# A hybrid decoder step on one Trainium2 core: post-norm weight products on GpSimd, and a longer first yield of decode

## The chip, the cores and the metric

The kernel runs on one core of one Trainium2 chip. The metric is the device time of one execution in microseconds (us), taken as the median of several runs. The engines are named as the profile names them: PE (TensorE, the matrix engine; its weight loads are PEld), DVE (VectorE), ACT (ScalarE), POOL (GpSimd) and SP (SyncE, which here only issues DMAs). All data are fp32; PE gets each fp32 operand as a high and a low part (tiles that end in `h` and `l`), so that one product in fp32 is three matmuls.

## The reference

One decoder layer, for a prompt of 2048 tokens (16 blocks of 128) and for 8 sequences of 4 new tokens each that continue from a stored state ("decode", 32 tokens, called the sample chunk):

```python
def rms_norm(x, g):
    y = xf * lax.rsqrt(jnp.mean(xf * xf, axis=-1, keepdims=True) + EPS)
    return (y * g.astype(F32)).astype(x.dtype)

def decoder_layer(x, p, lp, state):
    xn = rms_norm(x, lp['norm_mix_pre'])
    ... # one projection to both groups of heads: mLSTM and sliding-window attention
    mix = jnp.concatenate([y_m, y_a], axis=-1) @ lp['w_out']
    x = x + rms_norm(mix, lp['norm_mix_post'])
    u = rms_norm(x, lp['norm_ffn_pre'])
    f = jnp.square(jax.nn.relu(u @ lp['w_up'])) @ lp['w_down']
    x = x + rms_norm(f, lp['norm_ffn_post'])
    x = x + jax.nn.sigmoid(x @ lp['w_pgate']) * (p @ lp['w_pproj'])
```

The change concerns the factors `norm_mix_post` and `norm_ffn_post` of the two post-norms, and the place of decode's mLSTM and attention in the program.

## The kernel before

The first part (up to some 720 us) projects all blocks and runs the prompt's mLSTM and window attention. The second part goes over three groups, `gi` = 0, 1, 2, of two chunks each: blocks 0-2 and 3-5, 6-8 and 9-11, 12-13 and 14-15 (with the sample chunk in the last group). For each group stand, in this order: `mix_mm` of the first chunk (product with `w_out`, tiles `mo`), `mix_post` (residual, store to `x1d`, norm, transposes `ut<block>...t`), the same for the second chunk, then `mlp` in 16 steps (products `up`, squared ReLU, split into `hh` and `hl`, products `dn`, which DVE accumulates in `f` at L1728), and last the gate (`gate_embed`, `gate_post` with transposes `xt<block>...t`, `gate_mm` with tiles `pg` and `pv`, output put at L1810). The first two steps of `mlp` are direct products; from the third on `up_both` uses a Strassen-like scheme that needs sums of the chunks' operands. `sums()` and `last_sum()` (L1641 to L1675) make them on DVE and POOL, with ACT splitting off the high parts.

PE's order is set by the code: a class `Flow` issues matmuls in program order, and four side generators are advanced at each step of PE's model time. A `yield us` in a generator means that it goes on only once PE's issued work has grown by so many model microseconds. So a yield's number says how many products of the main line stand between two pieces of a side. The other engines' order follows from a scheduler that works from the same program and its dependences; each engine then runs its queue strictly in order. POOL's queue also issues DMAs.

`decode()` is one of the sides. It is added before `mix_mm` of the first chunk of group 1. It waits `DECW`, then runs `decode_mlstm` (loads of the state through POOL's queue: `cb`, `zqk`, `zg`, `hrow` and others, then at once the transposes `dph` of `hrow` and `zqk` on PE, later products `dpX`, `dpU`, `dpno`) and `decode_swa` (loads L1303 to L1321, products `daS`, transposes `daT` and `daTn`, copies to `spts`, products `daO`, then `sya` is scaled at L1384 to L1387 and put out). At the last direct step of group 1's `mlp` (s = 1), the line `pe.drain(dec)` (L1770) issues all that is left of it, before the pools for the sums are opened and `sums()` is added as a side.

`finished(b, half, g, scale)` is called for each half (512 columns) of a block's `f` as it gets complete: from `mix_mm` with `gpost`, from the last `mlp` step and from `gate_post` with `gffn`. It lets ACT sum the squares, and multiplies the half with the weights in place. The residual (L1449, two instructions on DVE) follows `rstd` (DVE L1454, POOL L1455 with a power of -1/2).

Of the kernel before, what the change touches and what calls it, by code (L numbers as in the profile page):

```python
# [14 lines left out]
ALU = mybir.AluOpType  # L15
# [41 lines left out]
TSP = 1.4  # L57
WBUF = 5
WIDE = 4
DECW = 5.0  # L60
DECF = 1.0
UPW = 7.0, 7.0
UPS = 2.8, 3.5
# [132 lines left out]
def hybrid_layer(ctx: ExitStack, tc: tile.TileContext, A, O):  # L196
    nc = tc.nc
    act, dve, pool = nc.scalar, nc.vector, nc.gpsimd
# [1191 lines left out]
    def decode():  # L1390
        yield DECW
        for dec in (decode_mlstm, decode_swa):
            with tc.tile_pool(name=dec.__name__, bufs=1, side="right", reuse_waits="tile") as sp:
                for us in dec(sp):
                    yield DECF * us
# [38 lines left out]
    def finished(b, half, g, scale):  # L1434

        n, nm = tok(b)
        if half == 0:
            ms[b] = small.tile([P, 6], F32, tag="ms", name=f"ms{nm}", bufs=8)
        v = f[b][:n, half * 512 : half * 512 + 512]
        junk = jp.tile([P, D], BF16, tag="j", name=f"j{nm}{half}", bufs=2)  # L1440
        act.activation(junk[:n, :512], v, AF.Square, scale=scale, accum_out=ms[b][:n, half : half + 1])  # L1441
        eng = (pool, dve)[half]
        eng.tensor_tensor(v, v, g[:n, half * 512 : half * 512 + 512], ALU.mult)  # L1443

    def residual(b, rs, x):
        n, nm = tok(b)
# [11 lines left out]
    def tok(b):  # L1458
        return (NS, "s") if b == "s" else (P, f"{b}")
# [46 lines left out]
    def mix_mm(gi, ci, c, sample):  # L1506
# [8 lines left out]
        for half in range(2):  # L1515
            hs = slice(half * 512, half * 512 + 512)
            for e in range(2):
                pss = [psum(ps_mm, f"mo{half}{e}{b}") for b in c]
                for k in range(4 * e, 4 * e + 4, 2):
                    w = [[t[:, :512] for t in w] for w in ring.take(2)]  # L1520
                    for i in range(len(c)):
                        for j in range(2):
                            mm3(pss[i], x.at(k + j, cols(i)), w[j], (k + j) % 4 == 0, (k + j) % 4 == 3)
                            pe.tick()
                    if sample:
                        if k == 0:
                            psS = psum(ps_o, f"mo{half}s")
                        for j in range(2):
                            mm2s(psS, sy[:, k + j], w[j], k + j == 0, k + j == KT - 1)
                for i, b in enumerate(c):  # L1530
                    if e == 0:
                        act.copy(f[b][:, hs], pss[i])
                    else:
                        dve.scalar_tensor_tensor(f[b][:, hs], pss[i], rsa[:, b : b + 1], f[b][:, hs], ALU.mult, ALU.add)
                        finished(b, half, gpost, 1.0 / 32)
            if sample:
                join_s(f["s"][:NS, hs], psS, 512, f"mo{half}")
                finished("s", half, gpost, 1.0 / 32)
# [50 lines left out]
    def mlp(gi, chunks, sample):  # L1589
# [141 lines left out]
        def down(s, ci, half, wd, hid):  # L1731
            c = chunks[ci]
            if sample and ci == 1:

                W = len(c) * P + NS
                names = [f"{half}t{m}" for m in range(4)]
                w = lambda m, ft: [t[:, m * P : (m + 1) * P] for t in wd[ft]]
                x = lambda m, ft: [t[:, :W] for t in hid[1, ft]]
                out = lambda m: f["t"][:, 4 * half + m]
            else:  # L1740
                names = [f"{half}{b}" for b in c]
                w = lambda i, ft: [t[:, cols(i)] for t in hid[ci, ft]]
                x = lambda i, ft: wd[ft]
                out = lambda i: f[c[i]][:, half * 512 : half * 512 + 512]
            for i in accumulate(s, ci, names, w, x, out, hid):
                if s == STEPS - 1 and not (sample and ci == 1):
                    finished(c[i], half, gffn, rq[:, c[i], 1:2])
                pe.tick()
# [230 lines left out]
```

## Time and profile before

| | |
|---|---|
| runs | 2670.22, 2674.26, 2679.49 us; median 2674.26 |
| profiled execution | 2676.5 us, its span 2674.7 us |
| mean granted TensorE clock | 0.981 |
| busy, of the span | PE 95%, PEld 83%, DVE 55%, ACT 36%, POOL 25% |
| instructions | PE 14260, DVE 3112, ACT 2165, POOL 936 |
| moved by DMA | 632.23 MB, mean 236 GB/s |

Times in the profile count from the span's start. A row of a timeline gives start and duration in us, engine, source line, operation, output<-inputs, shape and count; square brackets hold the engine's idle time just before it and what ended that. A row of a group (`L1443 POOL ... x16: a/b/c`) gives the minimum, median and maximum duration in ns. A row of the windows view gives a stretch, then each engine's busy time with its number of instructions, then the granted clock, the DMA engines' busy share and GB/s.

### The profile page before, as it was taken

What the parts mean: (1) busy time and instruction counts of PE and PEld (TensorE: products, weight loads), DVE (VectorE), ACT (ScalarE), POOL (GpSimd) and SP (SyncE); (2) the same over time, 40 slices, a digit from 0 to 9 for tenths busy, and PEclk for the clock granted to TensorE, in tenths of its full rate; (3) what the DMA queues carried; (4) which work ended last, traced back from release to release, by engine and by line L of the source; (5) the groups of instructions that cost most, each with busy time, mean ns of one, the idle gap of its engine ahead of it and who ended that gap; (6) DMA issues with size and microseconds to landing.
All of it is one profiled execution on the core that took longest, in us unless ns stands there. A gap on an engine that the chain in (4) does not pass through costs nothing.

```text
span 2674.7 us, 39114 instructions
## 1 busy us (share of the span) xinstructions
PE 2549.5 (95%) x14260; PEld 2212.9 (83%) x14260; DVE 1481.7 (55%) x3112; ACT 975.9 (36%) x2165; POOL 658.0 (25%) x936
## 2 busy tenths in 40 slices
PE   7899999998899999999998999999999998999998
PEld 6787878877688888888776789988888877999986
DVE  6675666664677655655735564444446345444443
ACT  5545344543455433444513432222223133222231
POOL 5311111111436666666513320000001012000010
PEclk9999999999999999999998999999999998999999
DMA  8765656666786666666987645555557885777786
GB/s 305 268 215 173 217 167 221 210 241 224 255 326 240 254 245 236 236 236 233 341 323 238 209 142 188 189 189 174 173 182 256 288 316 187 254 261 258 257 297 230
DMA packets 215186, 632.23 MB, mean 236 GB/s; under 512 B 24790, under 2 KB 58794, under 8 KB 214977
## 3 DMA queue, kind: packets, MB, share of 16 engines
q1 hardware_dynamic: 169552, 472.19, 52.0%
q0 software_dynamic: 45392, 157.50, 15.1%
q8 instruction: 113, 1.85, 0.3%
q14 instruction: 81, 0.66, 0.1%
q10 hardware_dynamic: 48, 0.03, 0.0%
HBM read 475.47 MB, written 155.25 MB: 236 GB/s over the span
## 4 chain that ended last, share of the span: by engine, by line
PE 74%; DVE 10%; DMA 6%; issue 4%; POOL 3%; ACT 2%; SPq 0%; POOLq 0%; DVEq 0%; ACTq 0%
PE dn L145 20%; PE up L145 20%; PE pg L145 5%; PE mo L145 5%; PE v L145 3%; DMA wk<-w 3%; PE qk L145 2%; DVE hl L229 2%; DMA w<-wk 2%; PE o L145 2%; PE gv L145 2%; PE qa L145 1%; PE aT L149 1%; PE aO L145 1%; PE pv L145 1%
## 5 line engine op out<-in xcount | busy, mean ns | idle before, releaser
L145 PE MATMUL dn<-w,hh 128*128 128x512 f32 x1792 | 566.6, 397 | 13.7 <-DVE f L1449 5.1
L145 PEld LDWEIGHTS dn<-w,hh 128*128 128x128 f32 x1792 | 333.2, 189 | 95.1 <-DVE f L1728 8.6
L1728 DVE TENSOR_TENSOR f<-f,dn 128x512 f32<-128x512 f32 x420 | 286.9, 687 | 222.0 <-PE dn L145 220.9
L145 PE MATMUL dn<-w,hl 128*128 128x512 f32 x896 | 355.5, 397 | 2.5 <-DVE hl L229 2.4
L1692 DVE TENSOR_TENSOR re<-up,re 128x384 f32<-128x384 f32 (+1 forms) x294 | 152.0, 517 | 326.4 <-PE up L145 326.4
L145 PEld LDWEIGHTS dn<-w,hl 128*128 128x128 f32 x896 | 169.0, 189 | 46.3 <-DVE hl L229 7.5
L1693 ACT COPY re<-up 128x384 f32<-128x384 f32 (+1 forms) x42 | 18.9, 450 | 414.8 <-PE up L145 414.8
L1617 ACT ACTIVATE re<-re 128x384 f32<-128x384 f32 (+1 forms) x168 | 83.2, 495 | 207.9 <-DVE re L1692 205.8
L229 DVE TENSOR_TENSOR hl<-re,hh 128x384 fp32r<-128x384 f32 (+1 forms) x192 | 137.7, 717 | 31.1 <-ACT hh L228 30.4
L275 POOL DMA_DIRECT2D wk<-w x242 | 134.0, 555 | 32.2 <-DVE w L250 29.2
L1443 POOL TENSOR_TENSOR f<-f,gffn 128x512 f32<-128x512 f32 x16 | 21.8, 1365 | 476.5 <-ACT j L1441 476.2
L250 POOL TENSOR_TENSOR w<-wr,w 128x512 fp32r<-128x512 f32 (+2 forms) x76 | 104.9, 1380 | 87.5 <-ACT w L249 86.6
L249 ACT CAST w<-wb 128x512 fp32r<-128x512 f32 x98 | 60.7, 621 | 173.2 <-PE dn L145 118.3
L249 ACT CAST w<-wr 128x512 fp32r<-128x512 f32 (+2 forms) x152 | 89.3, 598 | 85.6 <-PE up L145 34.3
L250 POOL TENSOR_TENSOR w<-wb,w 128x512 fp32r<-128x512 f32 x70 | 91.9, 1313 | 116.3 <-ACT w L249 115.8
L1618 ACT ACTIVATE re<-re 128x384 f32<-128x384 f32 (+1 forms) x192 | 95.1, 495 | 5.9
L228 ACT CAST hh<-re 128x384 fp32r<-128x384 f32 (+1 forms) x192 | 92.8, 483 | 6.8
L1043 ACT ACTIVATE s<-s,swt 128x257 f32<-128x257 f32 (+1 forms) x128 | 63.4, 497 | 77.5 <-DVE swt L1040 76.4
L1037 DVE CUSTOM_DVE_ANT_0 s<-aS,cst,sink 128x256 f32<-128x256 f32 (+1 forms) x128 | 57.0, 473 | 59.4 <-PE aS L145 59.2
L1624 POOL CAST hh<-hh 128x16 fp32r<-128x16 f32 x32 | 8.0, 249 | 319.0 <-ACT hh L228 319.0
L145 PE MATMUL up<-t0h,w 128*128 128x384 f32 (+1 forms) x336 | 85.1, 320 | 0.0
L145 PE MATMUL up<-t1h,w 128*128 128x384 f32 (+1 forms) x336 | 85.1, 320 | 0.0
(1537 smaller groups left out, 6530.7 us busy)
## 6 DMA issues: line engine op xcount, KB each, us to landing
w<-wk SPq DMA_DIRECT2D x692, 512.0 KB, 4.7
wk<-w POOLq DMA_DIRECT2D x238, 512.0 KB, 6.6
wr<-in_w_down_dram SPq DMA_DIRECT2D x64, 256.0 KB, 7.7
wb<-in_w_up_dram SPq DMA_DIRECT2D x28, 512.0 KB, 6.8
w<-wk SPq DMA_DIRECT2D x20, 528.0 KB, 4.4
x<-in_x_prompt_dram SPq DMA_DIRECT2D x16, 512.0 KB, 5.2
y<-yd SPq DMA_DIRECT2D x32, 256.0 KB, 7.1
xr<-in_x_prompt_dram SPq DMA_DIRECT2D x16, 512.0 KB, 6.3
```

Source lines behind the costliest of these rows:

```text
L145: ins = self.pe.matmul(out, lhsT, rhs, start=start, stop=stop)
L228: act.copy(hi, src)
L229: dve.tensor_tensor(lo, src, hi.bitcast(F32), ALU.subtract)
L249: act.copy(hi, src)
L250: (eng or weng()).tensor_tensor(lo, src, hi.bitcast(F32), ALU.subtract)
L275: here(put(self.kept[key], t.bitcast(U32)))
L1037: dve.tensor_tensor_reduce(s_[:, s, lo : 2 * P], pS[:, s, lo:], bias[:, j, lo:], 1.0 if s == 0 else 0.0625, sink[:, h : h + 1], ALU.add, A ...
L1043: act.activation(e_, e_, AF.Exp, bias=nm[:, s : s + 1], accum_out=sm[:, s : s + 1])
L1617: act.activation(t, src, AF.Relu)
L1618: act.square(t, t)
L1692: add = lambda out, a, b: dve.tensor_tensor(out, a, b, ALU.add)
L1728: dve.tensor_tensor(out(i), out(i), ps[i], ALU.add)
```

## The change

`finished` multiplies both halves on POOL, where half 0 was on POOL and half 1 on DVE. `DECW` goes from 5.0 to 12.0.

```diff
-DECW = 5.0
+DECW = 12.0
...
-        eng = (pool, dve)[half]
-        eng.tensor_tensor(v, v, g[:n, half * 512 : half * 512 + 512], ALU.mult)
+        pool.tensor_tensor(v, v, g[:n, half * 512 : half * 512 + 512], ALU.mult)
```

The line numbers from `finished` on are one less after the change (L1443 becomes L1442, L1641 becomes L1640, L1728 becomes L1727).

The first place is the start of decode on PE, in `mix_mm` of group 1's first chunk: `mo` are that product's tiles, `yt9t` to `yt11t` transposes for the second chunk's mix. Before:

```order
L145 MATMUL mo_14221<-w_14258,yt10h_13904 128x512 x2
L145 MATMUL mo_14221<-w_14258,yt10l_13906 128x512
L149 MATMUL dph<-ident,hrow 128x24
L149 MATMUL dph<-ident,zqk 128x32
L149 MATMUL dph<-ident,hrow 128x24
L149 MATMUL dph<-ident,zqk 128x32
```

After:

```order
L149 MATMUL yt11t<-ident,y_14240 128x128 x4
L145 MATMUL mo_14309<-w_14312,yt10h_13905 128x512 x2
L145 MATMUL mo_14309<-w_14312,yt10l_13907 128x512
L145 MATMUL mo_14309<-w_14314,yt10h_13905 128x512 x2
L145 MATMUL mo_14309<-w_14314,yt10l_13907 128x512
L145 MATMUL mo_14310<-w_14312,yt10h_13905 128x512 x2
L145 MATMUL mo_14310<-w_14312,yt10l_13907 128x512
L145 MATMUL mo_14310<-w_14314,yt10h_13905 128x512 x2
L145 MATMUL mo_14310<-w_14314,yt10l_13907 128x512
L145 MATMUL mo_14311<-w_14312,yt10h_13905 128x512 x2
L145 MATMUL mo_14311<-w_14312,yt10l_13907 128x512
L149 MATMUL dph<-ident,hrow 128x24
```

Nine groups of `mo` and the transposes `yt9t`, `yt10t` and `yt11t` have come in front of `dph`.

The second place is decode's end on PE, in step 0 of group 1's `mlp`. Before:

```order
L149 MATMUL daTn_15519<-ident,sss_15428 32x128
L145 MATMUL dn_15533<-w_15529,hh_15477 128x512 x2
L145 MATMUL dn_15533<-w_15529,hl_15478 128x512
L145 MATMUL dn_15537<-w_15529,hh_15477 128x512 x2
L145 MATMUL dn_15537<-w_15529,hl_15478 128x512
L145 MATMUL daO_15541<-svc,spts_15494 128x64 x8
L145 MATMUL daO_15541<-zkv,spts_15494 128x64
L145 MATMUL dn_15555<-w_15529,hh_15477 128x512 x2
L145 MATMUL dn_15555<-w_15529,hl_15478 128x512
L145 MATMUL dn_15533<-w_15531,hh_15525 128x512 x2
```

After (the `up` that follows is step 1's first):

```order
L145 MATMUL dn_15553<-w_15543,hh_15493 128x512 x2
L145 MATMUL dn_15553<-w_15543,hl_15494 128x512
L149 MATMUL daT_15578<-ident,sss_15509 128x128 x4
L149 MATMUL daT_15584<-ident,sss_15509 128x128 x4
L149 MATMUL daTn_15590<-ident,sss_15509 32x128
L145 MATMUL daO_15593<-svc,spts_15577 128x64 x8
L145 MATMUL daO_15593<-zkv,spts_15577 128x64
L145 MATMUL up_15622<-ut10h_14600,w_15569 128x384
```

Decode's last transposes and products now stand behind all `dn` of that step, drained right ahead of step 1's `up`.

The third place is POOL's queue around `decode_swa`'s loads, where the mix of group 1's second chunk (blocks 9 to 11) ends. Before:

```order
L1443 TENSOR_TENSOR f_14636<-f_14636,gpost_14215 128x512
L1443 TENSOR_TENSOR f_14637<-f_14637,gpost_14215 128x512
L1303 DMA out_dram<-snr 4x64
L1443 TENSOR_TENSOR f_14638<-f_14638,gpost_14215 128x512
L1303 DMA out_dram<-snr 4x64 x7
L1308 DMA bias_s<-in_const_b_dram 128x1056
L1310 DMA zqa<-zsd 32x512
L1312 DMA zkv<-zsd 32x256
L1316 DMA skc<-in_cache_swa_k_dram 128x8x128
L1317 DMA svc<-in_cache_swa_v_dram 128x8x128
L1321 DMA ssnk<-in_attn_sinks_dram 32x2x1 x4
L1455 TENSOR_TENSOR ms_14965<-ms_14965,nhalf 128x1
```

After:

```order
L1303 DMA out_dram<-snr 4x64 x8
L1308 DMA bias_s<-in_const_b_dram 128x1056
L1310 DMA zqa<-zsd 32x512
L1312 DMA zkv<-zsd 32x256
L1316 DMA skc<-in_cache_swa_k_dram 128x8x128
L1317 DMA svc<-in_cache_swa_v_dram 128x8x128
L1321 DMA ssnk<-in_attn_sinks_dram 32x2x1 x4
L1442 TENSOR_TENSOR f_14587<-f_14587,gpost_14215 128x512
L1442 TENSOR_TENSOR f_14588<-f_14588,gpost_14215 128x512
L1442 TENSOR_TENSOR f_14589<-f_14589,gpost_14215 128x512
L1454 TENSOR_TENSOR ms_14931<-ms_14931,nhalf 128x1
```

The three half-1 multiplications of that chunk stand behind the loads; the half-0 ones (not shown after) stay ahead of them.

## Prediction

> **What bounds the kernel now.** I read the shares of the engines first, then what TensorE (PE) waited for, then the places where the change acts, in order of time.
>
> ```profile
> PE 2549.5 (95%) x14260; PEld 2212.9 (83%) x14260; DVE 1481.7 (55%) x3112; ACT 975.9 (36%) x2165; POOL 658.0 (25%) x936
> PE 74%; DVE 10%; DMA 6%; issue 4%; POOL 3%; ACT 2%; SPq 0%; POOLq 0%; DVEq 0%; ACTq 0%
> PE dph L149 <- DMA hrow<-in_state_mlstm_conv_dram: 9.0, 1, 9.0
> PE xt10t L149 <- DVE xt00l L229: 2.9, 1, 2.9
> PE dpU L145 <- DVE skm L1275: 2.4, 1, 2.4
> PE dpX L145 <- issue: 2.3, 1, 2.3
> ```
>
> PE is busy 95% of the span and is 74% of the chain that ended last (second row). GpSimd (POOL) and VectorE (DVE) have room on average, so a multiplication that changes engine is worth something only where PE waits on one of them. The other rows are PE's waits (us in total, times, longest). The largest that the change touches is `dph`, decode's first transpose, which waits 9.0 us for a load. The next view shows it: PE, POOL's loads, then clock by stretch.
>
> ```profile
> 1403.96 0.40 PE L145 MATMUL mo<-w,yt10l 128*128 128x512 f32 x1
> 1413.38 0.27 PE L149 MATMUL dph<-ident,hrow 24*128 24x24 f32 x1 [9.03 <-DMA hrow<-in_state_mlstm_conv_dram]
> 1403.39 0.54 POOL L1810 DMA_DIRECT2D out_dram<-ot  x1 [3.77 <-DVE ot L1808]
> 1405.50 0.52 POOL L1129 DMA_DIRECT2D hrow<-in_state_mlstm_conv_dram  x1
> 1404.00:1414.00 10.00, 0.97 (x8) 0.65 (x7) 0.00 (x0) 0.28 (x1) 5.75 (x13) 0.65 0.62 197
> 1414.00:1420.00 6.00, 6.00 (x22) 4.61 (x22) 5.52 (x22) 1.81 (x3) 4.00 (x8) 0.50 0.30 58
> ```
>
> PE has nothing to do from 1404.36 to 1413.38, because `hrow` is issued on POOL only at 1405.50, behind an output write that waited for its data until 1403.39. The last row, with PE busy for all 6.00 us at a granted clock of 0.50, is the second half of the price: 6 us of work at half speed, 3.0 us more than at full speed. Together the place costs 12.0 us.
>
> **Term A: the longer first yield.** PE's order after the change has nine `mo` groups (three matmuls each) and twelve transposes (`yt9t` to `yt11t`) ahead of `dph` that stood behind it. POOL's order of the decode loads is as before, so `hrow` is issued at about the same time.
>
> ```profile
> 1398.63 0.62 PE L145 MATMUL mo<-w,yt10h 128*128 128x512 f32 x2
> 1399.33 0.62 PE L145 MATMUL mo<-w,yt10h 128*128 128x512 f32 x2
> 1420.54 0.69 PE L149 MATMUL yt11t<-ident,y 128*128 128x128 f32 x4
> 2618.43 0.80 PE L149 MATMUL xt150t<-ident,f 128*128 128x128 f32 x4 [4.14 <-DVE xt21l L229]
> 2619.80 1.20 PE L145 MATMUL pg<-w,xt20h 128*128 128x512 f32 x2
> 1578.38 0.73 PE L145 MATMUL dn<-w,hh 128*128 128x512 f32 x2 [2.31 <-ACT hh L228]
> ```
>
> One group takes 0.70 us (1398.63 to 1399.33) and four transposes about 0.5 (a row of 0.69 that overlaps the next start, 0.45 later). 9 x 0.70 + 3 x 0.5 = 7.8, so `dph` is due at 1404.36 + 7.8 = 1412.1. If `hrow` lands as before, by 1413.38, 1.3 us of the stall stay; but the weight stream now keeps running beside it, so it may land later, by 1416 at worst (an estimate: the 7.9 us from its issue to `dph`, plus a third). I take a stall of 2.5 us and no loss of clock: behind a stall of 2.31 us two matmuls took 0.73 us together, behind one of 4.14 us 1.20. A = -(12.0 - 2.5) = -9.5, between -6 (4 us and the slow clock again) and -12. [...]
>
> **Term B: decode's middle.** The waits at `dpX` and `dpU` are 4.7 us in all. In the new order other `mo` groups stand between decode's steps, none of the steps has gone: I take 3.7 left, B = -1, between -4 and +2.
>
> **Term C: the mix's end behind decode's second part.** In POOL's new order the three half-1 multiplications of group 1's second chunk stand behind the loads of `decode_swa`; before they were on DVE.
>
> ```profile
> 1490.40 0.27 PE L149 MATMUL dpno<-ident,snc 128*16 128x128 f32 x1
> 1501.93 2.15 POOL L1321 DMA_DIRECT2D ssnk<-in_attn_sinks_dram  x4
> 1506.07 0.68 DVE L1443 TENSOR_TENSOR f<-f,gpost 128x512 f32<-128x512 f32 x1
> L1443 POOL TENSOR_TENSOR f<-f,gpost x16: 1286/1298/1730, 722.7 to 2185.1; 128x512 f32<-128x512 f32 x16
> L1443 DVE TENSOR_TENSOR f<-f,gpost x16: 669/682/694, 738.3 to 2199.4; 128x512 f32<-128x512 f32 x16
> ```
>
> POOL is free of those issues at 1504.1, 13.7 us after `dpno`. Before, 23 `mo` groups (counted in the order) stood behind `dpno` (16 us), so the first half-1 block was ready later than that. Now 12 stand there (8.4 us): the multiplications wait some 5 us for POOL and then take 3 x 1.30 in place of 3 x 0.68. Part of it is covered by the first `up` products, which need only the earlier chunk. C = +2.4, between 0 (all covered) and +5 (none).
>
> **Term D: decode's end moves in front of the sums.** Before, nine `dn` groups of step 0 stood between decode's last product (`daO`) and the first `up` of step 1. After, decode is drained behind all of them. What waits for it is DVE: the sums of the Strassen-like steps (L1641 and on) stand on DVE behind the scaling of decode's result (L507, L1387).
>
> ```profile
> 1550.84 0.43 PE L145 MATMUL daO<-zkv,spts 32*128 32x64 f32 x2
> 1551.31 1.27 ACT L1384 ACTIVATE sya<-daO,sst 32x64 f32<-32x64 f32 x4 [2.00 <-PE daO L145]
> 1554.19 0.47 DVE L1387 TENSOR_SCALAR sya<-sya,dyat 32x512 f32<-32x512 f32 x1 [0.68 <-POOL dyat L508]
> 1554.59 0.94 DVE L1641 TENSOR_TENSOR ts<-ut11h,ut10h 128x768 f32<-128x768 f32 x1
> 1558.28 0.34 PE L145 MATMUL up<-ut10h,w 128*128 128x384 f32 x1
> 1559.89 0.96 DVE L1659 TENSOR_TENSOR t0l<-ts,t0h 128x768 fp32r<-128x768 f32 x1
> 1564.16 2.60 DVE L1659 TENSOR_TENSOR t1l<-ts,t1h 128x768 fp32r<-128x768 f32 x1
> 1555.00:1585.00 30.00, 24.94 (x128) 22.49 (x127) 29.90 (x23) 12.57 (x21) 17.18 (x8) 0.99 0.39 126
> 1585.12 0.68 DVE L1728 TENSOR_TENSOR f<-f,dn 128x512 f32<-128x512 f32 x1
> 1585.86 1.22 PE L145 MATMUL dn<-w,hh 128*128 128x512 f32 x2
> ```
>
> The chain from `daO`'s end (1551.27) to the first sum (1554.59) is 3.3 us. Before, sums began 3.7 us ahead of step 1's first `up` (1558.28); after, 3.3 us behind it: 7.0 us later against PE. From there to the first accumulation of step 1 (1585.12) DVE is busy throughout (the row of the window 1555 to 1585), and PE's fourth `dn` group (1585.86) waits for it, since three buffers hold `dn`. So the 7.0 appears on PE. It could be 3 if the order of DVE's work, which changes here, lets the accumulations in earlier, and 8.5 if POOL's sums stretch more of DVE's rows (2.60 us at 1564.16 where the same operation took 0.96 at 1559.89). The drain also shows the copies between `daT` and `daO` to PE: +1.3 (before, two `dn` groups, 1.4 us, stood there). D = +8.3, between +3 and +10.
>
> **Term E: the multiplications elsewhere.** 32 + 2 go from DVE to POOL: 34 x 0.68 = 23 us off DVE, 34 x 1.30 = 44 on POOL. For most PE is not waiting on either. The places that count are the ends of the groups, where residuals feed the next transposes:
>
> ```profile
> 1303.87 1.69 DVE L1443 TENSOR_TENSOR f<-f,gffn 128x512 f32<-128x512 f32 x1
> 1305.48 0.68 DVE L229 TENSOR_TENSOR xt00l<-xt00t,xt00h 128x512 fp32r<-128x512 f32 x1
> 1306.21 0.66 PE L149 MATMUL xt10t<-ident,f 128*128 128x128 f32 x4 [2.90 <-DVE xt00l L229]
> 2206.03 2.81 DVE L1449 SCALAR_TENSOR_TENSOR f<-f,ms,xr 128x512 f32<-128x512 f32 x4 [3.44 <-DMA xr<-in_x_prompt_dram]
> 1290.51 0.15 DVE L1799 TENSOR_TENSOR ms<-ms,rq 128x1 f32<-128x1 f32 x1
> 2606.33 1.29 POOL L1443 TENSOR_TENSOR f<-f,gffn 128x512 f32<-128x512 f32 x1
> 2606.40 1.24 DVE L1799 TENSOR_TENSOR ms<-ms,rq 128x1 f32<-128x1 f32 x1 [0.67 <-POOL ms L1455]
> ```
>
> At group 0's end the split `xt00l` that PE waits for stood behind a multiplication that took 1.69 us; in the new order nothing of that kind is ahead of it: -1.5. At group 2's mix the residual waits for a load until 2206.03 after 3.44 us of idle time, which cover the 1.2 us more on POOL. At the very end POOL's chain gets six multiplications (four on full blocks and two for the sample chunk) where it had three, 3 x 1.30 more, while DVE loses 3 x 0.68 from the queue in front of `xt150t`; I take nothing. E = -1.5, between -4 and +8.
>
> The sum: -9.5 - 1 + 2.4 + 8.3 - 1.5 = -1.3 us. The profiled execution took 2676.5 us, of which 2674.7 are the span; its median of three runs is 2674.26, 2.2 below. Taken against the median, 2673.0 us. The three runs spread by 0.17% either way, so 0.3% (8 us) is about what a measurement tells from no change.
>
> **The rivals.** (1) The sums' delay is absorbed: DVE takes the accumulations and splits earlier in its new order, D is +2 in place of +8.3 and C is 0. Then -1.3 - 6.3 - 2.4 = -10, 2664 us: faster. For it: most of the sums that fill DVE are needed only by steps behind the next. Against it: DVE is full in the whole stretch, so something has to give.
>
> (2) Slower: POOL holds up DVE. The row at 2606.40 is a 128x1 product that takes 1.24 us, where at 1290.51 the same took 0.15, while a POOL multiplication runs (2606.33 to 2607.62). If each block's residual at the chunk ends is held by the two POOL multiplications ahead of it, PE waits 2 x 1.30 - 2 x 0.68 = 1.2 us more there, and the next block's multiplication blocks the residual once more, 0.7; with five such ends exposed (three gate ends and two mixes) that is 9.5 us, and the -1.5 of E is lost: -1.3 + 9.5 + 1.5 = +9.7, 2684 us. It decides from four exposed ends on. Against it: only the last chunk's and group 0's end have PE waits of over 2.5 us on DVE in the rows above. [...]
>
> (3) The longer yield does not do what it says: `hrow` lands later by as much as `dph` is moved. Then A is only the 3 us of clock and some of the stall, -4, and the time is +4.2, 2678 us: within 0.3%. Against it: the issue on POOL is tied to the output write, which is fed by work ahead of both.
>
> **How the numbers follow.** The forecast, terms near their middle, has 0.37, rival (1) 0.35, rival (2) 0.20, rival (3) 0.08. Forecast and rival (3) lie within 0.3% but for 0.04 at the edges: same 0.41, faster 0.37, slower 0.22. The range: 2660 (rival (1) with A at -12 and B at -2: 2664 - 3.5) to 2686 (rival (2) with D at +10: 2684 + 1.7). The forecast's own range is 2666 to 2681.
>
> **What would show it.** A: PE's wait for `hrow` at about 1412 falls from 9.0 to some 2.5 us, and the granted clock behind it stays above 0.9. C: `ut90t` starts with a wait of some 2 us. D: the first L1640 sum starts 3 us behind step 1's first `up` and the first L1727 of that step some 34 us behind it. E: `xt10t` waits under 1.5 us. Wrong would be a D that isn't there (DVE with idle time from the sums to the first accumulation), or PE waits of over 2 us on DVE or POOL at the chunk ends that were none before.

## The result, and the profile after

The changed kernel takes 2703.02 us (median of 4 runs, 2699.76 to 2709.47) where the kernel before takes 2674.45 (4 runs). The ratio is 1.0109, with a 95% interval of 1.0083 to 1.0135. It is 29 us slower, beyond the upper end of the range. Its profiled execution took 2703.43 us, with a span of 2701.3 us, against 2676.5 and 2674.7 before.

The page after, in the parts that answer to the ones shown of before (engines; then PE's waits: us in total, times, longest):

```profile
PE 2560.3 (95%) x14260; PEld 2219.4 (82%) x14260; DVE 1468.7 (54%) x3078; ACT 975.7 (36%) x2165; POOL 697.7 (26%) x970
PE mo L145 <- DMA w<-wk: 9.2, 4, 5.4
PE dn L145 <- ACT re L1616: 7.5, 1, 7.5
PE xt150t L149 <- DVE xt21l L229: 5.4, 1, 5.4
PE xt70t L149 <- DVE xt10l L229: 4.0, 1, 4.0
PE pt2t L149 <- DVE pl L229: 3.5, 1, 3.5
PE pt8t L149 <- DVE pl L229: 2.4, 1, 2.4
```

DVE has 34 instructions fewer and 13 us less to do, POOL 34 more and 40 us more, and both are still far from full: the shares say nothing of the loss. The waits do. The 9.0 us at `dph` are gone, and in their place stand a wait for a weight load and several at the places where a residual or a split feeds PE: `pt2t` and `pt8t`, for which PE did not wait before, `xt70t` (1.8 us before) and `xt150t` (4.1 before).

The next rows give the steps of the prediction one by one, in the timeline of after: decode's first transpose, its last product, step 1's first `up`, the first sum and the first accumulation behind it.

```profile
1420.87 0.24 PE L149 MATMUL dph<-ident,hrow 24*128 24x24 f32 x1 [0.64 <-DMA hrow<-in_state_mlstm_conv_dram]
1410.00:1430.00 20.00, 18.89 (x93) 14.65 (x92) 15.17 (x49) 10.71 (x21) 11.32 (x23) 1.00 1.00 313
1566.10 0.43 PE L145 MATMUL daO<-zkv,spts 32*128 32x64 f32 x2
1566.46 0.44 PE L145 MATMUL up<-ut10h,w 128*128 128x384 f32 x1
1569.85 0.94 DVE L1640 TENSOR_TENSOR ts<-ut11h,ut10h 128x768 f32<-128x768 f32 x1
1593.82 1.22 PE L145 MATMUL dn<-w,hh 128*128 128x512 f32 x2 [7.52 <-ACT re L1616]
1599.10 0.68 DVE L1727 TENSOR_TENSOR f<-f,dn 128x512 f32<-128x512 f32 x1
```

The wait for `hrow` is 0.64 us and the granted clock there is 1.00. The first sum starts 3.4 us behind step 1's first `up`, where before it started 3.7 us ahead, and the first accumulation comes 32.6 us behind that `up` (26.8 before). Both of decode's effects are there at about the forecast sizes. So most of the 29 us come from elsewhere.

To find where, I compared in each profiled execution the starts of the same matmuls: how much later than before the first product of a stage starts, less how much later the first `mo` of the whole program starts (it varies by -3.8 to +1.6 us between executions, ahead of anything that was changed). Step 2 of `mlp` is the first Strassen-like one; the rows of the gates take the first `pg`. All figures are us, from the timelines of PE.

| first product of | after | e1 | e2 | e3 | e4 | e11 | e12 |
|---|---|---|---|---|---|---|---|
| group 0, step 2 | +10.4 | 0.0 | +9.6 | +9.5 | -0.2 | +10.3 | -1.2 |
| group 0, gate | +13.2 | +0.1 | +12.4 | +10.0 | +5.2 | +12.1 | -0.7 |
| group 1, mix | +12.1 | -0.8 | +11.2 | +9.2 | +4.3 | +11.3 | -1.2 |
| group 1, `up` | +9.9 | -11.3 | +13.0 | +2.8 | +2.9 | +11.3 | -9.3 |
| group 1, step 2 | +19.1 | -2.3 | +13.9 | +4.3 | +2.9 | +12.2 | -7.6 |
| group 1, gate | +23.8 | -2.3 | +18.7 | +4.3 | +7.6 | +15.5 | -8.2 |
| group 2, step 2 | +26.6 | -4.3 | +18.4 | +2.9 | +5.8 | +14.3 | -9.7 |
| PE's last | +30.3 | -4.1 | +22.4 | +2.9 | +9.3 | +17.0 | -9.0 |

(e1: the longer yield alone; e2: all products on POOL alone; e3, e4: only those behind the mix, or behind the MLP; e11: half 1 on POOL and half 0 on DVE; e12: decode's first loads early. The experiments follow.) The first 10 us of the loss arise in the mix of group 0, which the prediction's sum gave no price (its rival (2) put 1.9 us there).

### The profile page after: what moved, and what is told of

It is laid out like the page before. It is cut to its first block, busy times and chain, and to the rows that moved or that the text cites. A ratio compares the mean times of both kernels' runs of the same rounds, so it can differ in the third digit from the quotient of the medians.

```text
span 2701.3 us, 39107 instructions
## 1 busy us (share of the span) xinstructions
PE 2560.3 (95%) x14260; PEld 2219.4 (82%) x14260; DVE 1468.7 (54%) x3078; ACT 975.7 (36%) x2165; POOL 697.7 (26%) x970
## 4 chain that ended last, share of the span: by engine, by line
PE 40%; issue 3%; DVE 3%; POOL 2%; DMA 2%; ACT 1%; POOLq 0%; SPq 0%; DVEq 0%; ACTq 0%
PE up L145 14%; PE dn L145 13%; PE pg L145 4%; PE mo L145 2%; DMA w<-wk 1%; PE pv L145 1%; POOL f L1442 1%; DVE f L1448 1%; DMA out_dram<-ot 0%; DMA hrow<-in_state_mlstm_conv_dram 0%; POOL ms L1454 0%; PE dpU L145 0%; DMA bias_s<-in_const_b_dram 0%; DMA xr<-in_x_prompt_dram 0%; POOL out_dram L1809 0%
## 5 line engine op out<-in xcount | busy, mean ns | idle before, releaser
L145 PEld LDWEIGHTS dn<-w,hh 128*128 128x128 f32 x1792 | 335.0, 190 | 105.6 <-DVE f L1727 14.3
L1727 DVE TENSOR_TENSOR f<-f,dn 128x512 f32<-128x512 f32 x420 | 286.8, 686 | 221.3 <-PE dn L145 220.4
L145 PEld LDWEIGHTS dn<-w,hl 128*128 128x128 f32 x896 | 169.7, 189 | 47.5 <-DVE hl L229 8.6
L1442 POOL TENSOR_TENSOR f<-f,gffn 128x512 f32<-128x512 f32 x32 | 41.3, 1296 | 479.9 <-ACT j L1441 479.4
```

The source lines that it names most:

```text
L145: ins = self.pe.matmul(out, lhsT, rhs, start=start, stop=stop)
L1442: pool.tensor_tensor(v, v, g[:n, half * 512 : half * 512 + 512], ALU.mult)
L1727: dve.tensor_tensor(out(i), out(i), ps[i], ALU.add)
```

## The experiments

Ratios are medians against the kernel before, run on the same chip, with 95% intervals.

**e1, the longer yield alone.**

```diff
-DECW = 5.0
+DECW = 12.0
```

> Only the longer first yield (12.0); the products stay half on POOL, half on DVE. Theory: the two parts add. The changed kernel lost 28.6 us; its trace puts about 20 of them at places where only the products changed, and about 7 at the start of the sums of group 1, where decode ends later. So here the wait at dph goes (9.0 us to about 1, no slow clock behind it, -12), the rest of decode and its end give back about as much, and the sums start some 7 us late: 2678 to 2684 us. Rival: what decode gives back in the changed kernel is caused by the products on POOL, so that without them the gain at dph stays: 2664 to 2670 us.

Measured: 2676.39 us, ratio 1.0016 (1.0004 to 1.0027), some 4 us slower. In the profiled execution, a quick one (2673.53 us), the column e1 shows a gain of 10.4 us between group 1's mix and its first `up`, and a loss of 9.0 from there to step 2. So decode's end gives back what its start wins. The profiled pair alone would make e1 4.1 us faster (last row of its column); the medians make it slower, and which stage the 4 us sit in isn't shown.

**e2, all products on POOL alone.** The change's diff of `finished`, with `DECW` at 5.0.

> Only the products on POOL; the first yield stays 5.0. Theory: loss of some 20 us at the mix of group 0 (a weight load late by 5 us behind a residual load in SP's queue, and slow clock), at the gates' starts and at the end: 2692 to 2698 us, with PE's wait on a weight load of over 4 us near 755 us in the trace. Rival: the products cost little alone and the loss comes from both together: below 2684 us.

Measured: 2696.27 us, ratio 1.0089 (1.0068 to 1.0110). This part alone costs 24 us; with e1's 4 us it makes up the 29. The two parts add, within what the intervals can tell.

**e3 and e4, the two post-norms apart.** `DECW` at 5.0; e3 moves the half-1 products with `gpost`, e4 those with `gffn`.

```diff
-        eng = (pool, dve)[half]
+        eng = dve if half == 1 and g is gffn else pool    # e3; in e4: g is gpost
```

> First yield 5.0; of the products only those with the weights of the post-norm behind the mix go to POOL, those behind the MLP stay half and half. Theory: the loss of all products on POOL (+0.89%, 24 us) splits by place; its trace loses about 10 us at the mix of group 0 and about 4 at the mixes of groups 1 and 2: +0.4 to +0.65% over the kernel before. Rival: the residual loads' place in SP's queue comes from the MLP's products too, and the mix alone is free: within 0.2%.

> First yield 5.0; of the products only those with the weights of the post-norm behind the MLP go to POOL. Theory: what is left, at the starts of the three gates: +0.25 to +0.5% over the kernel before, with PE's waits pt2t, pt8t on DVE pl (3.5 and 2.4 us), xt70t and xt150t as with all products on POOL, and no weight wait near 755 us. Rival: these waits are made up for by the shorter ones at xt10t and xt20t: within 0.15%.

Measured: e3 2681.61 us, 1.0028 (1.0016 to 1.0040), below what was expected; e4 2683.98 us, 1.0041 (1.0027 to 1.0055), as expected. Together 0.69%, where e2 has 0.89% (0.68 to 1.10). The table shows the place: e3 loses as much as e2 in the mix of group 0 (9.5 and 9.6 us), nothing at the gates, and wins 6.4 us between group 1's mix and its `up`, where e2 loses 1.8. The clock, below (0.66 in e2 and 1.00 in e3, over 25 us), makes that difference between the two. The weight wait near 755 us is 5.8 us in e2 and in e3, and is absent in e4; e4 has the wait at `pt2t`:

```profile
1293.86 2.52 POOL L1443 TENSOR_TENSOR f<-f,gffn 128x512 f32<-128x512 f32 x2
1293.92 1.25 DVE L1799 TENSOR_TENSOR ms<-ms,rq 128x1 f32<-128x1 f32 x1 [0.36 <-POOL ms L1455]
1295.09 1.84 DVE L1449 SCALAR_TENSOR_TENSOR f<-f,ms,x 128x512 f32<-128x512 f32 x1
1298.53 0.41 DVE L229 TENSOR_TENSOR pl<-pt0t,ph 128x256 fp32r<-128x256 f32 x1
1298.99 0.69 PE L149 MATMUL pt2t<-ident,p 128*128 128x128 f32 x2 [3.48 <-DVE pl L229]
```

In e4's timeline DVE waits for POOL's power, which stands in POOL's queue between the products, and then a 128x1 product takes 1.25 us (0.16 at 1293.41) and half a residual 1.84 us (0.75 at 1289.23) beside the next two on POOL. What PE needs (`pl`) is queued behind that on DVE. How often DVE is held up like this shows in the 16 instances of that 128x1 product, first before, then e2, then e10 (all products on DVE, below); the three figures are the shortest, the median and the longest, in ns:

```profile
L1799 DVE TENSOR_TENSOR ms<-ms,rq x16: 147/155/1235, 1290.5 to 2610.5; 128x1 f32<-128x1 f32 x16
L1798 DVE TENSOR_TENSOR ms<-ms,rq x16: 145/1068/1250, 1300.6 to 2632.3; 128x1 f32<-128x1 f32 x16
L1799 DVE TENSOR_TENSOR ms<-ms,rq x16: 149/155/160, 1291.2 to 2607.4; 128x1 f32<-128x1 f32 x16
```

With no product on POOL none is held up; in e2 most are, and the 16 take 11.9 us in sum where before they took 5.4. DVE's idle time for POOL's power in front of them also grows, from 2.3 to 11.1 us.

**e6, four buffers instead of three for loads,** with both parts of the change.

```diff
-LBUF = 3
+LBUF = 4
```

> Both parts of the change, with four instead of three buffers for the loads of x, y and the residual's input. Theory: the residual load of group 0's second chunk does not stand before the weight loads waiting for a buffer, PE's wait of 5.4 us for a weight near 756 us and the slow clock behind it go, 7 to 9 us off the changed kernel: 2694 to 2697 us. Rival: the weight stream is late there for another reason (its buffers, the DMA share), the wait stays: 2701 to 2705 us.

Measured: 2699.93 us, ratio 1.0101 (1.0081 to 1.0122). By the time this can't be told from the changed kernel's 1.0109. The traces show what the weight wait is made of. `wk<-w` is POOL's store of a split weight to memory, `w<-wk` the load on SP that reads that copy back for the second chunk. The first row of each view is SP's wait for such a store from 728 to 760 us (us in total, times, longest); first before, then after, then e6:

```profile
SPq L282 <- DMA wk<-w: 2.1, 2, 1.1
740.27 0.67 DVE L1577 COPY cvo<-pcv 3x512 f32<-3x512 f32 x1
741.79 1.09 POOL L275 DMA_DIRECT2D wk<-w  x2
744.86 0.32 SPq L282 DMA_DIRECT2D w<-wk  x1
```

```profile
SPq L282 <- DMA wk<-w: 9.2, 2, 8.8
736.01 1.77 DVE L1448 SCALAR_TENSOR_TENSOR f<-f,ms,xr 128x512 f32<-128x512 f32 x1 [1.18 <-POOL ms L1454]
738.37 0.67 DVE L1576 COPY cvo<-pcv 3x512 f32<-3x512 f32 x1
739.33 0.62 POOL L1577 DMA_DIRECT2D out_dram<-cvo  x1 [2.10 <-DVE cvo L1576]
739.97 1.31 POOL L1442 TENSOR_TENSOR f<-f,gpost 128x512 f32<-128x512 f32 x1
741.21 1.15 POOL L275 DMA_DIRECT2D wk<-w  x2
739.73 0.33 SPq L1429 DMA_DIRECT2D xr<-in_x_prompt_dram  x1
749.87 2.02 SPq L282 DMA_DIRECT2D w<-wk  x4
756.28 1.22 PE L145 MATMUL mo<-w,yt01h 128*128 128x512 f32 x2 [5.35 <-DMA w<-wk]
```

```profile
SPq L282 <- DMA wk<-w: 7.9, 2, 5.3
735.98 1.70 SPq L1429 DMA_DIRECT2D xr<-in_x_prompt_dram  x3
743.57 1.16 POOL L275 DMA_DIRECT2D wk<-w  x2
750.08 0.32 SPq L282 DMA_DIRECT2D w<-wk  x1
756.90 0.73 PE L145 MATMUL mo<-w,yt01h 128*128 128x512 f32 x2 [1.79 <-DMA w<-wk]
```

Counted from the program's first `mo` in each execution (701.48, 697.73 and 702.61 us), the events are, in us:

| | before | after | e6 |
|---|---|---|---|
| DVE starts the copy `cvo` | 38.8 | 40.6 | 37.9 |
| POOL issues the first of the two stores | 40.3 | 43.5 | 41.0 |
| SP issues the load that waited for it | 43.4 | 52.1 | 47.5 |

After, a residual stands ahead of the copy `cvo` on DVE; it waits 1.18 us for POOL's power, and its first half takes 1.77 us beside a product on POOL, where the second took 0.73. The output of `cvo` is POOL's next issue, another half-1 product stands behind it, and only then come the two stores: 3.2 us later than before. They also take 8.7 us to land where it was 3.1; just ahead of them a residual's load `xr` and two weight loads went out, but what slowed them isn't separated. SP waits 8.8 us for the store, PE 5.35 us for the load behind it, and PE goes on at half clock (0.50 granted from 756 to 760 us, two matmuls in 1.22 us).

The theory of e6 was another: that the `xr` ahead of six weight loads, waiting for a buffer, holds them up. It does stand there, and waits until 739.73. But the two weight loads right behind it go out only about 1 us later than before (at 42.4 and 42.9 us behind the first `mo`, before at 41.3 and 42.0); the long wait is the next load's, for its store. With the fourth buffer `xr` is out before 738, the residual stands behind `cvo` on DVE, the stores go out 2.5 us earlier, PE waits 1.79 us and the two matmuls behind it take 0.73 us; the lateness of group 0's step 2 falls from 10.4 to 4.7 us. The effect on the time is not resolved.

**e5 and e9, an earlier end of decode.** e5 has both parts of the change and drains decode between the two `up` of step 0; e9 has the longer yield with the products as before, and drains it between the halves of step 0's second `dn`.

```diff
                 pe.drain(tsp)
+                if gi == 1:              # e5
+                    pe.drain(dec)
                 up(s, 1, wu, hid)
                 for half in range(2):
+                    if gi == 1 and half == 1:    # e9 in its place
+                        pe.drain(dec)
                     down(s, 1, half, down_weights(), hid)
```

> Both parts of the change, and in group 1 decode is drained already between the two up products of step 0, so that nothing of decode is left ahead of the sums. Theory: the sums start ahead of step 1's first up as before the change and PE's wait of 7.5 us on ACT re near 1594 goes: 6 to 9 us off the changed kernel, 2694 to 2697 us. Rival: DVE is full there in any case and only the place of the wait moves: 2701 to 2705 us.

> First yield 12.0, products half and half, and decode is drained in group 1 between the two halves of the second dn of step 0, so that half of those products stand between decode's last product and step 1's first up. Theory: against the longer yield alone (+0.16%) the 7 to 9 us at the start of the sums go: -0.05 to -0.2% against the kernel before. Rival: decode's chain has by then not enough other work between its steps (exp, copies), PE waits there instead: within 0.1% of the longer yield alone.

Measured: e5 2700.15 us, 1.0108 (1.0087 to 1.0129), no gain. The 7.5 us wait on `re` is gone, but PE now waits elsewhere: 4.7 us in all for the end of decode's own chain, as in the row of e5 below, and 5.1 us for copies of `dn` on ACT (L1725), which stand behind the sums' splits there. The rival was right: only the place of the wait moves.

```profile
1552.03 1.97 PE L149 MATMUL daT<-ident,sss 128*128 128x128 f32 x8 [2.45 <-ACT sss L1361]
```

e9: 2674.37 us, 1.0001 (0.9989 to 1.0012), against 1.0016 for the longer yield alone; the wait on `re` is 4.2 us where e1 has 7.4. That is towards the theory, but the two intervals overlap: inconclusive on the time.

**e8 and e12, decode's first loads early.** First yield 5.0 and products as before; two or four loads are issued before the first gate of group 0.

```diff
+        if gi == 0:
+            zq = lp.tile([NS, 512], F32, tag="zqk", name="zqk", bufs=1)
+            put(zq, zsd[:, Z_QK : Z_QK + 512])
+            ... # the same for hrow; in e12 also for zg and mps
         gate_mm(*part[0], first_ready)
```

> The kernel before (first yield 5.0, products half and half), but the two loads that decode's first transposes need, hrow and zqk, are issued before the first gate of group 0 into buffers of their own. Nothing else of decode moves. Theory: PE's wait of 9.0 us at dph and the slow clock behind it (12 us in all) go; with the order of decode's end as before, the sums do not start later, so what is gained stays, less the waits of the next steps of decode on their own loads: 6 to 12 us off, -0.22 to -0.45%. Rival: the next loads (cb, mps, scs), which sit at the same place of POOL's queue, make PE wait as long a little later: within 0.1%.

> The kernel before, with the four loads of decode's first steps (zqk, hrow, zg, mps) issued before the first gate of group 0; the run with two of them showed PE's wait moved from dph (9.0 us) to dpg (5.1 us, on zg). Theory: with zg there as well neither wait is left and the clock stays full at 1400 to 1420: 8 to 12 us off, -0.3 to -0.45%, less what a later step (dpX on the state's loads) takes. Rival: the wait moves on to the next load or to DVE's chain behind dpg: within 0.15%.

Measured: e8 2673.93 us, 1.0002 (0.9993 to 1.0012): the rival was right in that the wait moved on, in e8's timeline to `zg`, a load that it had not listed:

```profile
1413.22 0.26 PE L149 MATMUL dpg<-ident,zg 32*4 32x32 f32 x2 [5.09 <-DMA zg<-zsd]
```

e12 2666.32 us, 0.9961 (0.9948 to 0.9974). With four loads early neither of these two waits is left, PE is busy throughout and at full clock (1.00) where before it stood still (windows view of e12), and what is won stays, since the end of decode has not moved:

```profile
1400.00:1410.00 10.00, 10.00 (x56) 7.91 (x55) 5.14 (x17) 2.98 (x5) 4.81 (x12) 1.00 1.00 332
1410.00:1420.00 10.00, 10.00 (x44) 8.09 (x44) 9.37 (x29) 6.35 (x15) 5.54 (x10) 1.00 1.02 312
```

**e10 and e11, which half is on which engine.** First yield 5.0.

```diff
-        eng = (pool, dve)[half]
+        eng = dve                  # e10
+        eng = (dve, pool)[half]    # e11
```

> First yield 5.0, the opposite move: both halves' products on DVE, none on POOL. Theory (the cost comes from POOL's slow product standing between a block's last half and its residual, and from DVE instructions that POOL holds up): half 0 is done long before half 1 in the kernel before, so there is little to win, and the last MLP step has DVE accumulate at the same time: within 0.2%. Rival (every product on POOL costs, whichever half): as much won as the change lost for its 34, -0.4% or more.

> First yield 5.0, halves exchanged: half 0 on DVE, half 1 on POOL, so that POOL has as many products as in the kernel before, but the late ones. Theory (lateness counts: POOL's 1.30 us and its queue stand between the last half and the residual): most of the loss of all products on POOL, +0.5 to +0.9%. Rival (the number of products on POOL counts, by its busy time and by holding up DVE): within 0.2% of the kernel before.

Measured: e11 2691.74 us, 1.0058 (1.0043 to 1.0073). POOL has as many products as before, and two thirds of e2's loss is there: it matters that the late half is on POOL. Its column has most of that in the mix of group 0 (10.3 us) and 7.0 us at the gates, where e2 has 10.4. The weight wait near 755 us is back as well (5.2 us). It goes with the late `gpost` half on POOL: the five kernels with that half there and three buffers (after, e2, e3, e5, e11) wait 5.2 us or more; they issue the first of the two stores 42.9 to 43.8 us behind the first `mo` and load its copy from 51.6 us on. The eight with the half on DVE (before, e1, e4, e8, e9, e10, e12, e13) wait 0.4 us at most; their stores go out at 39.2 to 41.1 us and the copy is loaded by 43.6. e10 2670.27 us, 0.9978 (0.9967 to 0.9988): at the edge of what was expected, and half of what its rival asks for.

**e13, e12 and e10 together.**

> The four early loads and all products on DVE together, first yield 5.0. Theory: the two act at different places (decode's start in group 1; the residuals behind the mix and the MLP) and add: 0.9961 x 0.9978 = 0.9939, so 0.9925 to 0.9955 of the kernel before. Rival: they win at the same place or the slow clock takes one of them back: 0.996 or above.

Measured: 2668.08 us, 0.9968 (0.9955 to 0.9981). The rival's figure: the two gains don't add, and why isn't shown. e12 alone is as good, and the simpler one. Both beat the kernel before and the changed one.

## Why the prediction was wrong, by its own steps

**Term A, right at its place.** -9.5 was forecast with 2.5 us of the stall left; 0.64 was left, and the clock stayed at 1.00. That the load takes as long as before from its issue held (7.4 us to landing, 7.8 before). The reason given for the clock was wrong, though: that a stall of about 2.5 us costs none. In the trace of before the stall of 2.40 us at `dpU` is followed by half clock, 0.50:

```profile
1477.97 0.71 PE L145 MATMUL dpU<-sva,skm 32*128 32x130 f32 x4 [2.40 <-DVE skm L1275]
1480.00:1482.00 2.00, 2.00 (x7) 1.25 (x6) 0.00 (x0) 0.00 (x0) 0.00 (x0) 0.50 0.00 0
```

**Terms B and C, right in e1, not in the changed kernel.** In e1 the stretch from group 1's mix to its `up`, which holds A, B and most of C, won 10.4 us in the profiled execution; the sum of the three was -8.1. In the changed kernel's it won 2.2. There the waits of decode's middle are 3.8 us (3.7 forecast), but behind one of them the clock is 0.66 over 25 us, where e1 has 0.93, which B gave no price (last section). `ut90t` waits 0.83 us for the residual where some 2 us were forecast.

**Term D, right in size, its path in part.** +8.3 forecast, +9.0 in e1 and +9.2 in the changed kernel from the `up` to step 2. The sums started 3.4 us behind the `up` (forecast 3.3). But the long wait of PE, 7.52 us, is for ACT's `re`, which stood in ACT's queue behind a split that waited 3.72 us for a sum on POOL (L1652); only the 3.08 us behind it is for DVE's accumulation, the path that was forecast. A + B + C + D came to +0.2 us, and e1 measured about 4 (1 to 7).

**Term E is the step that failed.** It put the 34 products at -1.5 us, between -4 and +8; e2 measured 24. The sentence that failed is that for most of them PE is not waiting on POOL or DVE and that the places that count are the ends of the groups. By e2's column the 22 us of its profiled execution lie so: 9.6 at the mix of group 0, which had no price in the sum, 1.6 from there to group 1's mix (forecast -1.5), 2.7 across decode, 4.8 at group 1's gate, -0.3 through group 2's mix (forecast 0, right) and 4.0 from there to the end (forecast 0).

Three things are behind it. First, what else stands in POOL's queue: I counted the moved work on POOL and DVE and left out the stores of the weights, which SP's loads wait for. The late products on POOL send these stores out 3.2 us later, and PE waits for the weight. That is most of the 9.6, seen in five kernels and absent in eight. Second, the product on POOL lies on the chain from a block's last half to its residual, with POOL's queue in between; e11 shows that this, not the number of products, makes most of the cost. I had credited the DVE queue with losing a product ahead of `xt00l`. That came true, the 2.9 us wait at `xt10t` is gone; but the new order put a residual that waits for POOL ahead of other work, and PE waits 3.5 us at `pt2t` in its place. Third, rival (2), a DVE held up by POOL, is seen in the 128x1 products of e2 and e4 (1.07 us at e2's median, 1.25 us in e4's row, 0.16 us at the median before), and had the sign of the result. 34 products of 0.68 us would have taken 23 us off DVE; its busy time fell by 13.0, so other work on it took some 10 us longer. The rival priced the gates too low (1.9 us for each exposed end, where the three gates took 10.4 in all) and left out the stores; its 2684 us are 19 below the result. How the cost at the gates divides on PE between waiting in POOL's queue and being held up isn't separated by any run here. The prediction's own sign of being wrong, PE waits of over 2 us on DVE at the chunk ends that were none before, is there in `pt2t` and `pt8t`.

Rival (1), absorbed sums, and rival (3), a load that comes later by as much as `dph`, were both refuted, by the first sum's start at 1569.85 and by the 0.64 us left at `dph`.

## What to carry to other kernels

Count the change in every queue that it touches, and for everything that stands behind the moved work there: two stores, 3.2 us late behind a product, cost PE a weight wait of over 5 us, and the stage around it made up 9.6 of e2's 22 us. Here the operation that gates the next step was better on the engine that does it in 0.68 us than on the one that takes 1.30, though the averages said that the first is the fuller one. When a stall is due to a late load, try to bring the loads forward, all of them that the next steps need, before you move the work that waits: e12 won 0.39% by that, the longer yield nothing.

## What the runs showed of the hardware

The half clock behind a stall is not decided by its length alone. In e1 and in the changed kernel the same stall of 3.00 us stands at the same place of decode, first e1, then after, with the windows of 25 us behind each:

```profile
1475.53 0.71 PE L145 MATMUL dpU<-sva,skm 32*128 32x130 f32 x4 [3.00 <-DVE skm L1275]
1475.00:1500.00 25.00, 24.47 (x107) 19.55 (x108) 8.38 (x21) 3.94 (x9) 13.69 (x22) 0.93 0.66 207
```

```profile
1485.96 1.23 PE L145 MATMUL dpU<-sva,skm 32*128 32x130 f32 x4 [3.00 <-DVE skm L1275]
1485.00:1510.00 25.00, 24.04 (x75) 17.89 (x76) 4.39 (x12) 1.76 (x3) 8.95 (x15) 0.66 0.47 137
```

Behind it the granted clock is 0.93 in one and 0.66 in the other, 25 x (0.93 - 0.66) = 6.8 us of full-speed work. The same stall of 2.79 us in e2 and e3 (at 1485.81 and 1483.28) is followed by four matmuls in 1.19 and in 0.71 us, and over the next 25 us by a clock of 0.66 and 1.00: 8.5 us, about the 8.2 by which the two differ between group 1's mix and its `up`. What decides between the two isn't shown by these runs, and no length that is safe can be read from them: in the trace of before the clock stayed full behind 2.31 us (1.00 from 1578.38 to 1580.00), and fell behind 2.40 us (0.50 from 1480 to 1482) and behind 2.29 us at 1583.77 (0.54 from 1584.40 to 1586.40). So in a profiled execution alone, 6.8 to 8.5 us at one such stall can be the clock and not the change; differences of that size in the table's columns are to be read with this in mind, and the sizes of whole changes were read from medians.
